# Splitting a weight tile one engine operation at a time, and rebuilding a block of activations ahead of the other lanes of work

## The chip, the cores and the metric

The kernel runs on one core of one Trainium2 chip. The metric is the device time in microseconds (us) of one execution. The core has five engines that follow their own queues of instructions: PE (TensorE, the matrix products), DVE (VectorE), ACT (ScalarE), POOL (GpSimd) and SP, which here issues the transfers (DMA).

## The reference: what is computed

Two layers (`DEPTH = 2`) of a diffusion backbone with `D_MODEL = 1024` on 640 tokens, 128 of context and 512 latent ones. Cut to what matters:

```
h   = modulate(rmsnorm(x))                      # shift and scale from a map of SiLU(cond)
p   = h @ w_in                                  # columns split over four mixers
o   = concat(pool(p), neighbourhood_attention(p), retention(p), gla(p))
x  += gate * rmsnorm(o @ w_out)
h   = modulate(rmsnorm(x))
x  += gate * rmsnorm((silu(h @ w_g) * (h @ w_u)) @ w_down)
```

All of it is float32. Context tokens read only context; latent tokens start their scans from the final context states.

## The kernel before

**Products.** The 640 tokens stand in the free dimension as two halves of 320 (`HW`), the 1024 channels as eight blocks of 128 partitions (`h0` to `h7`). A float32 operand is held as two rounded parts, hi and lo, in a tile whose second index is 0 or 1; a product takes three matmuls of 128x320 for each 128x128 block of weights: hi by hi, hi by lo and lo by hi. So every weight tile that arrives from memory (`raw`, 512 KB) has to be split before PE can use it: a copy makes hi in `hl[:, 0]`, a subtraction makes lo in `hl[:, 1]`. A step of the bulk work is three such matmuls. In the gate and up products of the FFN (feed-forward network) seven products of sums stand in for eight (`seven`); their weights are sums of quarters of two raw tiles, which four operations make in place (`raw<-raw`) ahead of the copy and the subtraction. A half-sized split has the name `hu`.

**Who decides the order.** The program is written out at build time by Python generators. A planner (`Clock`) keeps, in its own units, until when each engine is planned. `drive` goes round: every lane (a generator of small work, such as one head of a mixer, a norm, or the boundary between two layers) makes one step, unless the planner has DVE or ACT booked beyond the present by more than `BACKLOG = 2500.0`; then `stream.feed()` may split the next weight tile; then the bulk (the dense products) makes one step. The order of the steps is the order of the instructions in each engine's queue. For each subtraction `vg` chooses between DVE and POOL, for each copy `copy` chooses between DVE and ACT, by the planner's state at that moment. So a change of when a step is made changes also which engine does what behind it.

**The stream of weights.** `Stream.load` starts transfers into three raw tiles. `Stream.split` issues all operations of one split at once: two, or six where sums are made. `Stream.feed` decides whether to split now; `Stream.next`, called by the bulk when it needs the tile, splits at once if that has not happened yet.

**The names that matter here.** `z` is the sum of the FFN's or the output projection's partial products (`z<-z,acc` adds a product from PSUM and so frees its tile for PE); `sg`, `u`, `act` are the FFN's gate, up and activation; `sq`, `ssqz` are squares and their sums for a norm, `nps` the norm's product over channels, `r` its inverse root; names that begin with `g` belong to GLA, with `n` to the neighbourhood attention, with `r` (`ro`, `rg`, `rq`) to retention; `hps` is a group norm's product. `boundary` ends a layer and makes the next one's `h` (first `xl<-z,nps`, then the modulation of `xl`, then `h` as hi and lo). `second_block` rebuilds, in the last group of the FFN, the second half of `h0` to `h3` from sums that stood there; it is a lane of 16 steps, and the bulk waits for its flag (`until(("block", l))`) before it uses the second half.

Every operation goes through a recording helper, so all rows name the line of that helper (L234 before, L235 after); the tiles' names tell them apart.

Of the kernel before, what the change touches and what calls it, by code (L numbers as in the profile page):

```python
# [133 lines left out]
BIAS_SMALL = -1000.0  # L134
BIAS_QBD = -400.0
BIAS_CP = -200.0
BIAS_SUM = 0.0
BIAS_SNAP = 400.0
BIAS_START = (-2000.0, 2000.0)
# [195 lines left out]
def emit(ctx, tc, a, o):  # L335
    nc = tc.nc
    clock = Clock()
    V, S, G, PE = (clock.proxy(n, e) for n, e in (("V", nc.vector), ("S", nc.scalar), ("G", nc.gpsimd), ("PE", nc.tensor)))
# [19 lines left out]
    def vg(out, in0, in1, op, bias=BIAS_VG):  # L358
        port = not clock.psum([in0, in1])
        if not port:  # L360
            V.tensor_tensor(out=out, in0=in0, in1=in1, op=op)
            return
        at = max(clock.now(), clock.avail(in0), clock.avail(in1))
        v = clock.free_at("V", port, at) + clock.cost("V", "tensor_tensor", [out], [in0, in1], {})
        g = clock.free_at("G", True, at) + clock.cost("G", "tensor_tensor", [out], [in0, in1], {})
        e = V if v <= g + bias else G
        e.tensor_tensor(out=out, in0=in0, in1=in1, op=op)
# [29 lines left out]
    def spawn(gen, first=False):  # L397
        lanes.insert(0 if first else len(lanes), [gen, 0.0, first])
# [198 lines left out]
    class Stream:  # L597


        def __init__(self):  # L600
            self.raw, self.hl, self.where = {}, {}, {}
            self.nd = self.nr = self.ns = self.nu = 0
            self.limit = 0
            self.used = [0, 0, 0]
            self.size = [3, 5, 2]

# [6 lines left out]
                self.nd += 1  # L613

        def split(self, at_once=False):
            kind, srcs, ends, where, _ = jobs[self.ns]
            self.used[where] += 1
            raw = self.raw[srcs[-1]]
            _, kt, n = items[srcs[-1]]
            if kind == "second":  # L620
                hl = hx[0].tile([128, 2, KT // 2, n], F32R, tag="hu", name="hu", bufs=self.size[2])
                raw = raw[:, KT // 2:]
            else:
                hl = (hx[0] if where else ring).tile([128, 2, kt, n], F32R, tag="hl", name="hl", bufs=self.size[where])
            if kind == "sums":

                g, u = self.raw[srcs[0]], raw
                (g1, g2), (u1, u2) = ((t[:, 0:KT // 2], t[:, KT // 2:]) for t in (g, u))
                for out, x, y, op in ((u2, u1, u2, ALU.add), (u1, g1, u1, ALU.subtract), (g1, u2, g1, ALU.subtract), (g2, g2, g1, ALU.subtract)):
                    vg(out, x, y, op, BIAS_SUM)  # L630
                raw = g
            copy(hl[:, 0], raw, BIAS_VS if at_once else bias[0][0])
            vg(hl[:, 1], raw, hl[:, 0].bitcast(F32), ALU.subtract, 2000.0 if at_once else bias[0][1])
            self.hl[self.ns] = hl
            self.where[hl.tensor.name] = where
            self.ns += 1
            for _ in range(ends):
                self.raw.pop(self.nr)
                self.nr += 1
            self.load()  # L640

        def free(self):
            where, when = jobs[self.ns][3:]
# [5 lines left out]
        def feed(self):  # L649

            self.load()
            if self.loaded() and self.free():
                now = clock.now()
                if clock.avail(self.raw[jobs[self.ns][1][-1]]) <= now + AHEAD and (
                        self.ns - self.nu < 2 or max(clock.t["V"], clock.t["S"]) <= now + BACKLOG):
                    self.split()

        def next(self):
            self.load()
            while self.ns <= self.nu:  # L660
                assert self.free() and self.loaded()
                self.split(True)
            hl = self.hl.pop(self.nu)
            self.nu += 1
            return hl
# [780 lines left out]
    def bulk():  # L1446
# [45 lines left out]
        tb0 = mod_mm(loads.pop(0))  # L1492
        V.tensor_tensor(out=xh(0, 0), in0=xh(0, 0), in1=rr[0], op=ALU.mult)
        V.tensor_tensor(out=xh(1, 0), in0=xh(1, 0), in1=rr[0], op=ALU.mult)
        stream.split()
        mod_end(*order[0], tb0)
        rest(rss[1])
        tb1 = mod_mm(loads.pop(0))
        V.tensor_tensor(out=xh(0, 1), in0=xh(0, 1), in1=rr[1], op=ALU.mult)
        mod_end(*order[1], tb1)  # L1500
        stream.split()
        V.tensor_tensor(out=xh(1, 1), in0=xh(1, 1), in1=rr[1], op=ALU.mult)
        for half in range(2):
            for k in range(2):
# [59 lines left out]
        for l in range(DEPTH):  # L1564
# [413 lines left out]
            for gi, gn in enumerate(GROUPS):  # L1978
# [48 lines left out]
                if last:  # L2027
                    if l == 0:
                        yield from until("mods1")
                    hpool("c", 5)  # L2030
                    free(6)
                    yield from room(2)
                    spawn(second_block())
                    sz = u5([128, 4, HW], "ssqz")
                    ssqs = [[sz[:, i], sz[:, 2 + i]] for i in range(2)]

                    hls = [(stream.next(), stream.next()) for _ in range(2)]
                    hds = []
                    for half in range(2):
                        if half:  # L2040
                            yield from until(("block", l))
                        for k in range(2):
                            yield from ev_ffn(*hls[k], acts[early + k], half)
                            if half:
                                stream.done(*hls[k])
                        if half:
                            lnexp()
                        for i in range(4):
                            if not half:
                                hds.append(stream.next())  # L2050
                            jobs = [(hds[i], 2 * i + m, half) for m in range(2)]
                            if i == 0:
                                yield from dn(jobs)
                            else:
                                for job in jobs:
                                    yield from dn([job])
                            if half:
                                stream.done(hds[i])
                        if half == 0:
                            xls = yield from residual(0, xsrc)  # L2060
                            spawn(boundary(0, zt, ssqs[0], xls, dst, nxt))
                else:
                    for i in range(4):
                        if len(z4) == i:
                            yield from room(1)
                            z4.append(u5([128, 2, TOK], "z"))
                        hl = stream.next()
                        jobs = [(hl, 2 * i + m, half) for m in range(2) for half in range(2)]
                        if i == 0:
                            yield from dn(jobs)  # L2070
                        else:
                            for job in jobs:
                                yield from dn([job])
                        stream.done(hl)
# [137 lines left out]
```

## Time and profile before

| | |
|---|---|
| median of 3 runs | 1692.34 us (1687.68 to 1692.91) |
| profiled execution, time | 1690.33 us |
| its span, first to last instruction | 1688.2 us |
| PE busy | 1598.9 us, 95% |
| DVE busy | 1269.9 us, 75% |
| ACT busy | 637.6 us, 38% |
| POOL busy | 307.4 us, 18% |
| mean granted clock of PE | 0.986 |

The span is 2.1 us shorter than the profiled execution's time, and that time is 2.0 us under the median. PE is the engine to watch: what the change can win or lose is PE's idle time, 1688.2 - 1598.9 = 89.3 us, and the stretches in which its clock is granted at the lower level.

### The profile page before, as it was taken

What the parts mean: (1) busy time and instruction counts of PE and PEld (TensorE: products, weight loads), DVE (VectorE), ACT (ScalarE), POOL (GpSimd) and SP (SyncE); (2) the same over time, 40 slices, a digit from 0 to 9 for tenths busy, and PEclk for the clock granted to TensorE, in tenths of its full rate; (3) what the DMA queues carried; (4) which work ended last, traced back from release to release, by engine and by line L of the source; (5) the groups of instructions that cost most, each with busy time, mean ns of one, the idle gap of its engine ahead of it and who ended that gap; (6) DMA issues with size and microseconds to landing.
All of it is one profiled execution on the core that took longest, in us unless ns stands there. A gap on an engine that the chain in (4) does not pass through costs nothing.

```text
span 1688.2 us, 31042 instructions
## 1 busy us (share of the span) xinstructions
PE 1598.9 (95%) x12400; PEld 1485.6 (88%) x12400; DVE 1269.9 (75%) x2510; ACT 637.6 (38%) x1396; POOL 307.4 (18%) x328
## 2 busy tenths in 40 slices
PE   4999999999999999999989998898999999999996
PEld 2888888999998998999979986778999999999996
DVE  5488767788677878786884588766786878878776
ACT  5346655664311112120543466646643211212132
POOL 0200142033011202010243000331330022111012
PEclk9999999999999999999999998999999999999998
DMA  9332231452454455221441311113421212222222
GB/s 368 129 123 93 95 103 63 162 164 82 158 200 162 172 179 183 97 96 63 135 149 58 102 46 42 50 40 132 139 80 65 74 63 101 80 71 92 71 82 94
DMA packets 80000, 188.15 MB, mean 111 GB/s; under 512 B 7632, under 2 KB 38256, under 8 KB 79856
## 3 DMA queue, kind: packets, MB, share of 16 engines
q1 hardware_dynamic: 79856, 186.17, 32.4%
q8 instruction: 98, 1.61, 0.4%
q14 instruction: 46, 0.38, 0.1%
HBM read 173.42 MB, written 12.71 MB: 110 GB/s over the span
## 4 chain that ended last, share of the span: by engine, by line
PE 71%; DVE 19%; ACT 4%; issue 3%; DMA 2%; POOL 1%; SPq 0%; DVEq 0%; ACTq 0%; POOLq 0%
PE acc L234 52%; PE acct L234 6%; DVE hl L234 5%; PE mps L234 3%; DVE z L234 2%; DVE sg L234 2%; DVE act L234 2%; DVE raw L234 1%; PE nsp L234 1%; PE nps L234 1%; DVE u L234 1%; PE rops L234 1%; DMA raw<-in_wdn 1%; PE gdps L234 1%; ACT sq L234 1%
## 5 line engine op out<-in xcount | busy, mean ns | idle before, releaser
L234 PE MATMUL acc<-h,hl 128*128 128x320 f32 x4800 | 764.8, 314 | 17.4 <-ACT h L234 8.4
L234 PEld LDWEIGHTS acc<-h,hl 128*128 128x128 f32 x4800 | 714.5, 189 | 46.5 <-issue 19.1
L234 PE MATMUL acc<-act,hl 128*128 128x320 f32 x2112 | 323.2, 313 | 12.1 <-DVE z L234 9.0
L234 PEld LDWEIGHTS acc<-act,hl 128*128 128x128 f32 x2112 | 314.5, 190 | 21.2 <-issue 11.5
L234 DVE TENSOR_TENSOR hl<-raw,hl 128x1024 fp32r<-128x1024 f32 (+1 forms) x204 | 251.4, 1241 | 12.6 <-ACT hl L234 8.5
L234 ACT ACTIVATE hl<-raw 128x1024 fp32r<-128x1024 f32 (+1 forms) x115 | 116.7, 1029 | 95.2 <-PE acc L234 44.8
L234 ACT ACTIVATE sg<-sg 128x320 f32<-128x320 f32 x64 | 30.2, 472 | 295.9 <-DVE sg L234 295.9
L234 PE MATMUL acct<-hl,h 128*128 128x256 f32 x960 | 132.4, 290 | 0.0
L234 PEld LDWEIGHTS acct<-hl,h 128*128 128x128 f32 x960 | 119.6, 191 | 8.3 <-issue 6.8
L234 PE MATMUL acc<-th,hl 128*128 128x320 f32 x768 | 118.7, 309 | 1.4 <-DVE hl L234 1.4
L234 PEld LDWEIGHTS acc<-th,hl 128*128 128x128 f32 x768 | 114.0, 188 | 2.4 <-DVE hl L234 1.9
L234 POOL TENSOR_TENSOR hl<-raw,hl 128x1024 fp32r<-128x1024 f32 (+1 forms) x24 | 60.2, 2508 | 256.6 <-ACT hl L234 246.9
L234 DVE CAST hl<-raw 128x1024 fp32r<-128x1024 f32 (+1 forms) x113 | 88.0, 779 | 20.1 <-PE acc L234 18.8
L234 DVE TENSOR_TENSOR z<-z,acc 128x320 f32<-128x320 f32 x160 | 71.3, 480 | 25.0 <-PE acc L234 24.7
L234 DVE TENSOR_TENSOR raw<-raw 128x512 f32<-128x512 f32 x103 | 71.0, 689 | 18.3 <-POOL raw L234 15.7
L234 POOL TENSOR_TENSOR raw<-raw 128x512 f32<-128x512 f32 x25 | 33.7, 1347 | 257.5 <-DVE hu L234 157.4
L234 POOL TENSOR_TENSOR nB<-nT,cst 128x248 f32<-128x248 f32 (+2 forms) x32 | 20.0, 624 | 279.9 <-DVE nsp L234 147.1
L234 DVE TENSOR_TENSOR u<-u,acc 128x320 f32<-128x320 f32 x96 | 46.4, 483 | 29.9 <-PE acc L234 27.6
L234 PE MATMUL acc<-th,hu 128*128 128x320 f32 x384 | 61.6, 309 | 0.0
L234 PEld LDWEIGHTS acc<-th,hu 128*128 128x128 f32 x384 | 57.6, 188 | 0.4 <-issue 0.4
L234 PE MATMUL mps<-mraw,ct 128*32 128x256 f32 x768 | 54.0, 391 | 2.0 <-DVE z L234 1.3
L234 ACT ACTIVATE hu<-raw 128x512 fp32r<-128x512 f32 x31 | 19.4, 626 | 91.8 <-PE acc L234 52.9
(284 smaller groups left out, 1976.0 us busy)
## 6 DMA issues: line engine op xcount, KB each, us to landing
mraw<-in_wmod SPq DMA_DIRECT2D x96, 512.0 KB
raw<-in_wgu SPq DMA_DIRECT2D x88, 512.0 KB
raw<-in_win SPq DMA_DIRECT2D x44, 512.0 KB
raw<-in_wdn SPq DMA_DIRECT2D x32, 512.0 KB
raw<-in_wout SPq DMA_DIRECT2D x16, 512.0 KB
xl<-xd SPq DMA_DIRECT2D x12, 640.0 KB
raw<-in_wdn SPq DMA_DIRECT2D x16, 384.0 KB
xd<-y SPq DMA_DIRECT2D x32, 160.0 KB
```

The costliest lines, as they stand in the source:

```text
L234: x = fn(*args, **kw)
```

## The change

`split` becomes a generator that yields after every operation. `feed` makes one of its steps in each round of `drive`, between the lanes' steps and the bulk's step, and a split that has begun goes on only while neither DVE nor ACT is planned beyond the present by more than `STEP = 2500.0`. `next` runs what is left. The two splits at the start of the program are made whole as before (`whole`). And `second_block` becomes the first lane of the list, which is also exempt from the limit on the backlog.

```diff
+STEP = 2500.0
...
+            self.cur = None
...
                 for out, x, y, op in ((u2, u1, u2, ALU.add), (u1, g1, u1, ALU.subtract), (g1, u2, g1, ALU.subtract), (g2, g2, g1, ALU.subtract)):
                     vg(out, x, y, op, BIAS_SUM)
+                    yield
                 raw = g
             copy(hl[:, 0], raw, BIAS_VS if at_once else bias[0][0])
+            yield
             vg(hl[:, 1], raw, hl[:, 0].bitcast(F32), ALU.subtract, 2000.0 if at_once else bias[0][1])
...
+            self.cur = None
             self.load()
+
+        def step(self, at_once=False):
+            if self.cur is None:
+                self.cur = self.split(at_once)
+            next(self.cur, None)
...
         def feed(self):
 
             self.load()
-            if self.loaded() and self.free():
-                now = clock.now()
+            now = clock.now()
+            if self.cur is not None:
+                if max(clock.t["V"], clock.t["S"]) <= now + STEP:
+                    self.step()
+            elif self.loaded() and self.free():
                 if clock.avail(self.raw[jobs[self.ns][1][-1]]) <= now + AHEAD and (
                         self.ns - self.nu < 2 or max(clock.t["V"], clock.t["S"]) <= now + BACKLOG):
-                    self.split()
+                    self.step()
+
+        def whole(self):
+            n = self.ns
+            while self.ns == n:
+                self.step()
...
             while self.ns <= self.nu:
-                assert self.free() and self.loaded()
-                self.split(True)
+                assert self.cur is not None or (self.free() and self.loaded())
+                self.step(True)
...
-        stream.split()
+        stream.whole()
...
-        stream.split()
+        stream.whole()
...
-                    spawn(second_block())
+                    spawn(second_block(), True)
```

The numbers of matmuls and of operations on weights stay the same; what moves is their order and, by the planner's choices, their engine. Over the whole program POOL has 25 subtractions `hl<-raw,hl` of 128x1024 in place of 21, 7 `hu<-raw,hu` in place of 3, 23 sums `raw<-raw` in place of 25; DVE has 187 such `hl` subtractions in place of 191.

DVE in layer 1, at the end of the first group of `seven` products of the FFN, where the adding of the down products to `z` begins. Before:

```order
L234 TENSOR_TENSOR act_14571<-sg_14827,act_14571 128x320
L234 TENSOR_TENSOR hl_14957<-raw_14852,hl_14957 128x1024
L234 TENSOR_TENSOR hu_14969<-raw_14863,hu_14969 128x512
L234 TENSOR_TENSOR raw_14863<-raw_14863 128x512
L234 TENSOR_TENSOR raw_14863<-raw_14852,raw_14863 128x512
L234 TENSOR_TENSOR raw_14852<-raw_14863,raw_14852 128x512
L234 TENSOR_TENSOR raw_14852<-raw_14852 128x512
L234 CAST hl_14975<-raw_14852 128x1024
L234 TENSOR_TENSOR hl_14975<-raw_14852,hl_14975 128x1024
L234 TENSOR_TENSOR z_14293<-z_14293,acc_14950 128x320
L234 TENSOR_TENSOR z_14293<-z_14293,acc_14951 128x320
```

And now (buffer numbers differ, the place is the same):

```order
L235 TENSOR_TENSOR act_14570<-sg_14826,act_14570 128x320
L235 TENSOR_TENSOR hl_14956<-raw_14848,hl_14956 128x1024
L235 TENSOR_TENSOR hu_14968<-raw_14859,hu_14968 128x512
L235 TENSOR_TENSOR raw_14859<-raw_14859 128x512
L235 TENSOR_TENSOR raw_14859<-raw_14848,raw_14859 128x512
L235 TENSOR_TENSOR raw_14848<-raw_14859,raw_14848 128x512
L235 TENSOR_TENSOR raw_14848<-raw_14848 128x512
L235 CAST hl_14977<-raw_14848 128x1024
L235 TENSOR_TENSOR z_14292<-z_14292,acc_14949 128x320
L235 TENSOR_TENSOR z_14292<-z_14292,acc_14950 128x320
L235 TENSOR_TENSOR z_14292<-z_14292,acc_14951 128x320
```

The subtraction of the split with the sums (`hl_14975`, now `hl_14977`) has left DVE; it stands in POOL's queue, where before the next tile's subtraction (`hl_15052`) stood, which in turn is DVE's now. The third group of the same layer changes in the same way.

ACT at the boundary between layer 0 and layer 1. Before:

```order
L234 ACTIVATE ssqz<-z 128x320
L234 ACTIVATE r_9546<-nps,cst 128x320
L234 ACTIVATE r_9545<-r_9546 128x320
L234 ACTIVATE ssqz<-z 128x320
L234 ACTIVATE sq<-z 128x320 x4
L234 ACTIVATE r_9546<-r_9545 128x320
L234 ACTIVATE sq<-z 128x320 x2
L234 ACTIVATE ssqz<-z 128x320
L234 ACTIVATE hl<-raw 128x1024
L234 ACTIVATE xl<-xl,modt_82,der_83 128x128
L234 ACTIVATE xl<-xl,modt_82,der_83 128x192
L234 ACTIVATE h_123<-xl 128x320
```

And now:

```order
L235 ACTIVATE r_9531<-nps,cst 128x320
L235 ACTIVATE r_9530<-r_9531 128x320
L235 ACTIVATE r_9531<-r_9530 128x320
L235 ACTIVATE ssqz<-z 128x320
L235 ACTIVATE sq<-z 128x320 x6
L235 ACTIVATE xl<-xl,modt_82,der_83 128x128
L235 ACTIVATE ssqz<-z 128x320
L235 ACTIVATE hl<-raw 128x1024
L235 ACTIVATE h_123<-xl 128x320
```

The square that ends the inverse root (`r_9546<-r_9545`, now `r_9531<-r_9530`) has moved ahead of five squares of the second half's products, and one of the two modulations of `xl` is no longer ACT's; the six squares still stand ahead of the first `h`.

DVE in the mixing of layer 0, at one of the splits of the input projection. Before, one split's two operations stand next to each other:

```order
L234 TENSOR_SCALAR rk_1672<-acc_1724 128x320
L234 TENSOR_TENSOR gE_1748<-gE_1748,gqk_232 128x512
L234 COPY qbd0_810<-gE_1748 32x256 x2
L234 COPY_PREDICATED gD_1658<-msk_76,gdps_1800 128x256
L234 CAST hl_1815<-raw_1382 128x1024
L234 TENSOR_TENSOR hl_1815<-raw_1382,hl_1815 128x1024
L234 STREAM_TRANSPOSE modb_1844<-mps_1835 128x256
```

And now there are 46 rows between the copy and the subtraction (`rq_1962<-acc_2059` takes the product that PE makes just before it first uses `hl_1898`):

```order
L235 COPY_PREDICATED gD_1684<-msk_76,gdps_1880 128x256
L235 CAST hl_1898<-raw_1337 128x1024
L235 SCALAR_TENSOR_TENSOR r1_1843<-hps_1840,r1_1843 128x256
...
L235 COPY_PREDICATED gD_2114<-msk_76,gdps_2148 128x128
L235 TENSOR_SCALAR rq_1962<-acc_2059 128x320
L235 TENSOR_TENSOR hl_1898<-raw_1337,hl_1898 128x1024
L235 TENSOR_TENSOR gE_2158<-gE_2158,gqk_232 128x256
```

The subtraction has moved from right behind its copy to right behind the eviction of the product before its own.

The programs can also be compared as a whole. For each split one counts the matmuls on PE between the last product whose eviction stands ahead of the split's last operation and the split's first use. Of 260 splits before, the smallest count is 24, the median 150.5, and 6 are under 40; now the smallest is 1 (`hl_1898`), the next are 11, 13, 27, 28 and 29, the median is 144, and 10 are under 40. In layer 1's mixing, the stretches of PE's queue in which only GLA and attention products stand, with no dense product among them, were 25 and 25 rows long and are now 10 and 35. In the output projection of layer 1 ACT's rows `h<-po` to `h<-go` stand directly behind `rg<-rg`, ahead of the two `hl<-raw` that stood there, DVE's two `hl<-raw,hl` ahead of `ro<-ro,rg` are gone from there and two copies `h<-no` have come to DVE; the last group norm's product on PE stands 18 matmuls earlier.

## Rows read from the trace of the kernel before

**Rows 1.** The page: busy time of each engine, share of the span, instructions.

```profile
span 1688.2 us, 31042 instructions
...
PE 1598.9 (95%) x12400; PEld 1485.6 (88%) x12400; DVE 1269.9 (75%) x2510; ACT 637.6 (38%) x1396; POOL 307.4 (18%) x328
```

**Rows 2.** The page: the chain that ended last, by engine.

```profile
PE 71%; DVE 19%; ACT 4%; issue 3%; DMA 2%; POOL 1%; SPq 0%; DVEq 0%; ACTq 0%; POOLq 0%
```

**Rows 3.** The page's costliest groups: count, busy us, mean ns, idle before them, its releaser.

```profile
L234 DVE TENSOR_TENSOR hl<-raw,hl 128x1024 fp32r<-128x1024 f32 (+1 forms) x204 | 251.4, 1241 | 12.6 <-ACT hl L234 8.5
...
L234 POOL TENSOR_TENSOR hl<-raw,hl 128x1024 fp32r<-128x1024 f32 (+1 forms) x24 | 60.2, 2508 | 256.6 <-ACT hl L234 246.9
...
L234 DVE TENSOR_TENSOR z<-z,acc 128x320 f32<-128x320 f32 x160 | 71.3, 480 | 25.0 <-PE acc L234 24.7
```

**Rows 4.** Windows, PE alone: stretch, length, PE busy (instructions), granted clock, DMA share.

```profile
60.00:300.00 240.00, 238.07 (x2232) 1.00 0.28 91
...
1016.00:1041.00 25.00, 17.83 (x171) 0.80 0.14 45
1053.00:1068.00 15.00, 11.33 (x85) 0.89 0.35 113
```

**Rows 5.** Timeline of DVE around 1350, and a later CAST: start, us, operation, count.

```profile
1348.94 2.79 DVE L234 CAST hl<-raw 128x1024 fp32r<-128x1024 f32 x1
1351.76 1.23 DVE L234 TENSOR_TENSOR hl<-raw,hl 128x1024 fp32r<-128x1024 f32 x1
...
1410.58 0.69 DVE L234 CAST hl<-raw 128x1024 fp32r<-128x1024 f32 x1
```

**Rows 6.** Timeline of POOL, and of PE with its idle time before and the releaser.

```profile
1348.70 2.48 POOL L234 TENSOR_TENSOR hl<-raw,hl 128x1024 fp32r<-128x1024 f32 x1 [29.41 <-ACT hl L234]
...
1354.72 1.55 PE L234 MATMUL acc<-act,hl 128*128 128x320 f32 x9 [2.47 <-DVE z L234]
...
1491.19 1.59 PE L234 MATMUL acc<-act,hl 128*128 128x320 f32 x9 [2.75 <-DVE z L234]
```

**Rows 7.** Timeline of PE at the boundary between the layers.

```profile
870.11 0.64 PE L234 MATMUL acc<-h,hl 128*128 128x320 f32 x1 [6.20 <-ACT h L234]
871.98 0.90 PE L234 MATMUL acc<-h,hl 128*128 128x320 f32 x2 [1.23 <-POOL h L234]
```

**Rows 8.** Timeline of ACT there.

```profile
861.99 0.46 ACT L234 ACTIVATE r<-r 128x320 f32<-128x320 f32 x1
...
867.69 1.04 ACT L234 ACTIVATE hl<-raw 128x1024 fp32r<-128x1024 f32 x1
868.64 0.92 ACT L234 ACTIVATE xl<-xl,modt,der 128x128 f32<-128x128 f32 x2
869.59 0.47 ACT L234 ACTIVATE h<-xl 128x320 fp32r<-128x320 f32 x1
```

**Rows 9.** Timeline of PE in layer 1's mixing, the longest waits.

```profile
1023.62 1.08 PE L234 MATMUL gdps<-qbd,gE 128*32 128x128 f32 x16 [2.52 <-ACT qbd L234]
...
1036.13 1.98 PE L234 MATMUL gops<-gat,gv 128*64 128x128 f32 x16 [2.61 <-ACT gat L234]
...
1094.41 0.53 PE L234 MATMUL ntp<-cst,nS 128*96 128x128 f32 x3 [2.26 <-ACT nS L234]
```

**Rows 10.** Timeline of PE at the output projection of layer 1.

```profile
1156.15 0.42 PE L234 MATMUL acc<-h,hl 128*128 128x320 f32 x1 [2.18 <-ACT h L234]
1158.87 1.43 PE L234 MATMUL acc<-h,hl 128*128 128x320 f32 x4 [2.30 <-DVE h L234]
```

**Rows 11.** Timeline of DVE there.

```profile
1152.83 2.36 DVE L234 TENSOR_TENSOR hl<-raw,hl 128x1024 fp32r<-128x1024 f32 x2 [0.57 <-ACT hl L234]
1155.11 0.89 DVE L234 TENSOR_TENSOR ro<-ro,rg 128x320 f32<-128x320 f32 x2
```

**Rows 12.** Timeline of PE in dense products; a window as in Rows 4.

```profile
899.83 4.42 PE L234 MATMUL acc<-h,hl 128*128 128x320 f32 x29
...
870.00:875.00 5.00, 3.66 (x8) 0.50 0.66 209
```

## The prediction, made before the changed kernel ran

> **What bounds the kernel.** I read the page's first section, the chain, the costliest groups, PE's windows, then the timelines of PE and of the engines that release it. PE is busy for 1598.9 of 1688.2 us [rows 1] and holds 71% of the chain that ended last, DVE 19%, ACT 4% [rows 2]. The matmuls don't change in number, so the change can only work on PE's 89.3 us of idle time and on the clock behind it. Where that time lies is to be seen stage by stage: in the mixing of layer 0, from 60 to 300 us, PE is busy for 238.07 of 240 us at a granted clock of 1.00 [rows 4], and nothing can be won there. The waits are short ones elsewhere: 2.47 and 2.75 us at two of the points where the FFN's down products begin [rows 6], 6.20 + 1.23 us at the boundary between the layers [rows 7], 7.17 and 3.67 us in two stretches of layer 1's mixing (length less busy time [rows 4]), 2.26 us later in it [rows 9], 2.18 + 2.30 us at layer 1's output projection [rows 10]. These are 30.8 us, and each of them ends with a small operation on DVE, ACT or POOL that stood behind work on weights or behind its own chain. I go through them by what the order of the changed program puts there.
>
> **Term 1, the two z points of layer 1: -5.2 us.** PE waits for DVE to add a finished product to z and so to free its tile. DVE comes to it late, since a CAST of weights takes 2.79 us there and a subtraction of 1.23 us follows [rows 5]; an ordinary CAST takes 0.69 us [rows 5]. The long one runs beside a POOL subtraction of 2.48 us that began 0.24 us before it and ended at 1351.18, 0.55 us before the CAST did [rows 5, 6]: it waited for POOL. Now the subtraction that follows the CAST is POOL's and can't begin before the CAST ends, and the one that POOL had there is DVE's, behind the z. So the CAST should take 0.69 us (2.10 won) and the subtraction is gone from ahead of z (1.23 won): 3.3 us, more than either wait, 2.47 and 2.75 [rows 6], so both go. POOL then works for 2.5 us beside the additions to z; these have one operand in PSUM, and their group shows 480 ns in the mean over 160 [rows 3], so I cost that at nothing. If they were held up the gain would be 0; the bounds are 0 and -5.2.
>
> The Trainium skill, page "SBUF — State Buffer", section "Who interferes with whom", has the same as a rule: whichever of a DVE copy in its two-port mode and a GpSimd operation starts first has the shared pair of ports for its whole length, and the other fully blocks. The trace agrees at this place (2.79 against 0.69 us). By that rule the change can also lose: it is the third rival.
>
> **Term 2, the boundary: -1 us.** The first product of layer 1 waits 6.20 us for the first h on ACT, then 1.23 us for its lo on POOL [rows 7]. The square that completes the inverse root comes at 861.99 [rows 8], and the change makes it early. But the first h then still stands behind the six squares, the last sum of squares and a weight copy, which ended at 867.69 + 1.04 = 868.73; only the 0.92 us of modulation between that and 869.59 [rows 8] are off ACT's path. That gives 869.59 - 868.73 = 0.9 us, rounded to 1. Bounds: 0 and -7.4, all of the wait.
>
> **Term 3, GLA in layer 1's mixing: -3 us.** While only small GLA and attention matmuls stand in PE's queue, PE waits for their chain through ACT and DVE, 2.52 and 2.61 us at a time [rows 9], and at a granted clock of 0.80 in the mean [rows 4]. The two stretches had 25 rows each, and cost 7.17 / 25 = 0.29 and 3.67 / 25 = 0.15 us of idle time a row. They now have 10 and 35: -15 x 0.29 + 10 x 0.15 = -2.8, rounded to -3. Bounds: -7.2, the first stretch's idle time gone, and +1.5, only the lengthening.
>
> **Term 4, attention at 1094 us: -1.2 us.** PE waits 2.26 us for a score's softmax on ACT [rows 9]. The lane of this head is some rows further ahead in the new order; I take half, with bounds of 0 and -2.3.
>
> **Term 5, the output projection of layer 1: -3.3 us.** The two waits are for h, on ACT and on DVE [rows 10]. On DVE a wait of 0.57 us and two subtractions of weights, 2.36 us, stand ahead of the gating of the retention's output [rows 11]; both are gone from there, and two copies of h have come to DVE, which at ACT's time for the same shape, 0.47 us [rows 8], is some 0.9 less the overlap, say 0.7: 2.93 - 0.7 = 2.2. The norm's product that starts this chain stands 18 matmuls earlier, which at the pace of 4.42 / 29 = 0.152 us each [rows 12] is 2.7 us and could take the rest. I take the middle of 2.2 and 4.48. Bounds: 0 and -4.5.
>
> **Term 6, splits that end late: +3 us.** Now a split that has begun stops between its operations as long as the planner has DVE or ACT booked ahead. Before, no split ended with fewer than 24 matmuls (3.6 us at 0.152) between it and its first use. Now six stand at 1, 11, 13, 27, 28 and 29. For `hl_1898` PE has to end the product, DVE evicts it (0.48, as z) and subtracts (1.24) [rows 3]: 1.7 us, with nothing to cover them; this is in layer 0's mixing, where PE never waited before. Three have 27 to 29 matmuls, 4.1 us and more, which cover 1.7; the two with 11 and 13 have 1.7 and 2.0 us, which just cover it. I add 1.3 us for operations that queue between: +3. Bounds: 0, and six times the worst that rows show: eviction 0.48 and a POOL subtraction of 2.51 [rows 3], 3.0 us, plus 0.75 us of lower clock, as the window behind the boundary's wait ran at 0.50 [rows 12]: +22.5.
>
> **The block first: 0.** In both layers its first operation stands one place earlier on DVE. The bulk's wait for the block shows no row of its own among PE's waits, since a half of products covers it.
>
> **Sum.** -5.2 - 1 - 3 - 1.2 - 3.3 + 3 = -10.7 us. The profiled execution before took 1690.33 us, 2.1 more than its span; so 1679.6 on its scale, and with the 2.0 us by which it lies under the median, 1681.6.
>
> **Rivals.** A: the waits only move. Speaks for it: in mixing and at the boundary PE waits for a chain of small operations, 2.5 us at a time [rows 9], whose links are as long as before; what leaves one stretch of the queue turns up in the next (10 and 35 rows). Then terms 2 to 5 are 0, and -5.2 + 3 = -2.2 gives 1690. Against it: in term 5 weights do stand in the way on DVE, as rows and not as a chain. B, slower: late splits stall PE at each of the six places, for 3.75 us. Terms 1 to 5 are -13.7; 22.5 - 13.7 = +8.8, 1701. It decides from 13.7 / 3.75 = 3.7, that is four stalls on; five make it slower by what can be measured. For it: `hl_1898` has one matmul of cover, and 10 splits instead of 6 have fewer than 40. Against it: a median of 144 matmuls, near 22 us of cover. C: POOL, with four more subtractions of 128x1024 and four more of half that size, holds up DVE's copies, each by 2.1 us as in rows 5 or about 1.3 by halving POOL's 2.51 us: 4 x 2.1 + 4 x 1.3 = 13.6, if each fell before something that PE waits for; 13.6 - 10.7 = +2.9, 1695. Against it: DVE is busy for 75% [rows 1] and in most places has time to catch up.
>
> **Chances.** My forecast 0.55; A 0.22; B 0.15; C 0.08. A measurement of this kernel can tell about 0.3%, 5.1 us, from no change. My forecast's own range is 1668 (the sum with terms 2 to 5 near their better ends, -24) to 1687 (5.1 under the median). The range that holds 8 in 10 goes from 1668 to 1697, which takes in A and C and the start of B. Faster by over 0.3%: 0.57, the forecast and a little of A; within 0.3%: 0.25, most of A and C; slower: 0.18, B and a little of C.
>
> **What would show it.** Term 1: PE's waits for z in the first and third group of layer 1's FFN are gone and no CAST there takes over 1 us; a CAST of 2.8 us ahead of z would refute it. Term 2: PE's wait at the boundary is about 5 us, not 6.2. Terms 3 and 5: less than 8 us idle in the two GLA stretches together, under 1.5 us at the output projection. Term 6: waits for `hl` among PE's, of 1 to 2 us, first in layer 0's mixing, where PE was busy throughout; if they sum to over 10 us, B holds. The prediction is wrong if PE's idle time doesn't fall by about 10 us from 89.3, or if its busy time rises since the lower clock is granted in longer stretches.

## The result, and the profile after

The changed kernel takes 1682.14 us in the median of 4 runs (1680.16 to 1683.00), against 1692.62 us before: a ratio of 0.9945 (95% interval 0.9932 to 0.9958), faster by 10.5 us in the medians (the ratio by itself is 9.3 us). The forecast was 1681.6 us. That the two are so close is partly luck: two terms of the sum came as said, two were a little larger, one failed, layer 0 lost three times the 3 us that the prediction had put down for losses, and a gain in the FFNs that it did not have made up for these.

The page's first section of the kernel after (compare [rows 1]):

```profile
span 1678.4 us, 31025 instructions
...
PE 1595.3 (95%) x12400; PEld 1482.1 (88%) x12400; DVE 1280.1 (76%) x2505; ACT 632.8 (38%) x1401; POOL 307.9 (18%) x326
```

The span is 9.8 us shorter: PE's idle time fell by 6.2 us (89.3 to 1678.4 - 1595.3 = 83.1), and its busy time by 3.6 us for the same 12400 matmuls, since its clock is at the lower level for less time (mean granted clock 0.989, before 0.986). PE's waits after, by what ended them (total us, times, longest):

```profile
PE acc L235 <- POOL hl L235: 6.1, 2, 3.0
PE gops L235 <- ACT gat L235: 5.5, 4, 2.5
PE acc L235 <- ACT h L235: 5.4, 1, 5.4
PE gdps L235 <- DVE qbd L235: 4.9, 3, 2.5
PE acc L235 <- DVE z L235: 4.3, 3, 1.8
...
PE acct L235 <- DVE hl L235: 2.0, 3, 0.8
...
PE acc L235 <- DVE hl L235: 1.0, 1, 1.0
```

And two groups of them before:

```profile
PE acc L234 <- DVE z L234: 9.0, 4, 2.7
...
PE acc L234 <- DVE hl L234: 1.4, 2, 0.7
```

The waits for `hl`, a split's subtraction that is not done when PE wants the tile, have grown from 1.4 to 6.1 + 2.0 + 1.0 = 9.1 us.

To see where the time went, I number the 9024 matmuls of the dense products in order of time, which is the same in all these kernels up to small exchanges, and compare the start of the n-th in two traces. The differences between one n and a later one are the gain or loss of a stage. In us, after less before:

| stage (dense matmuls) | us |
|---|---|
| start and mixing of layer 0 (to 1125) | +6.6 |
| its output projection, first FFN group (to 2000) | +2.7 |
| rest of its FFN, boundary (to 4750) | -4.2 |
| mixing and output projection of layer 1 (to 6375) | -5.5 |
| FFN of layer 1 (to the end) | -9.4 |
| sum | -9.8 |

One profiled execution stands behind each side. Where two kernels have the same queues, the start of the program differed by up to 1.6 us and the stages behind it by up to 1.1, so smaller differences mean nothing. The expectations further down have +7.3, +2.9 and -5.8 us for the changed kernel's +6.6, +2.7 and -5.5: they count from the first dense product and cut at slightly other places.

Timeline of DVE and POOL at the first z point of layer 1, and of PE (compare [rows 5, 6]):

```profile
1348.56 0.69 DVE L235 CAST hl<-raw 128x1024 fp32r<-128x1024 f32 x1
1349.17 2.86 DVE L235 TENSOR_TENSOR z<-z,acc 128x320 f32<-128x320 f32 x7
1351.95 1.22 DVE L235 TENSOR_TENSOR hl<-raw,hl 128x1024 fp32r<-128x1024 f32 x1
...
1349.48 2.42 POOL L235 TENSOR_TENSOR hl<-raw,hl 128x1024 fp32r<-128x1024 f32 x1 [30.57 <-DVE hl L235]
...
1341.16 11.02 PE L235 MATMUL acc<-act,hl 128*128 128x320 f32 x74
```

The CAST takes 0.69 us in place of 2.79, z follows at once, and PE goes through 74 matmuls with no wait. POOL's 2.42 us lie beside seven additions to z at 2.86 / 7 = 0.41 us each, which are not held up. At the other point, in the third group, the CAST takes 0.69 us too and PE's wait is gone. A third wait for z, near the end of this FFN, stays: 1.93 us before, 1.24 us now.

The boundary between the layers, PE and ACT (compare [rows 7, 8]):

```profile
874.62 0.64 PE L235 MATMUL acc<-h,hl 128*128 128x320 f32 x1 [5.44 <-ACT h L235]
876.32 0.90 PE L235 MATMUL acc<-h,hl 128*128 128x320 f32 x2 [1.06 <-POOL h L235]
...
872.79 0.47 ACT L235 ACTIVATE ssqz<-z 128x320 f32<-128x320 f32 x1 [1.70 <-DVE z L235]
873.17 1.04 ACT L235 ACTIVATE hl<-raw 128x1024 fp32r<-128x1024 f32 x1
874.11 0.45 ACT L235 ACTIVATE h<-xl 128x320 fp32r<-128x320 f32 x1
```

Windows of PE (length, busy, granted clock, DMA share; compare [rows 4]):

```profile
60.00:300.00 240.00, 232.08 (x2183) 1.00 0.27 91
...
1016.00:1041.00 25.00, 23.34 (x260) 1.00 0.21 66
1053.00:1068.00 15.00, 11.23 (x90) 0.89 0.23 81
```

In layer 0's mixing PE, busy for 238.07 us before, is busy for 232.08: 6 us of new idle time. In layer 1's the stretch from 1016 is full now, but its GLA waits stand elsewhere. Waits of PE in both mixings and at the ends of the output projections (compare [rows 9, 10]):

```profile
150.66 0.64 PE L235 MATMUL gdps<-qbd,gE 128*32 128x128 f32 x16 [1.59 <-DVE qbd L235]
...
183.25 0.41 PE L235 MATMUL acc<-h,hl 128*128 128x320 f32 x1 [0.99 <-DVE hl L235]
...
394.14 3.83 PE L235 MATMUL acc<-h,hl 128*128 128x320 f32 x13 [3.03 <-POOL hl L235]
...
999.91 1.18 PE L235 MATMUL gops<-gat,gv 128*64 128x128 f32 x16 [2.52 <-ACT gat L235]
...
1062.21 0.66 PE L235 MATMUL gdps<-qbd,gE 128*32 128x128 f32 x8 [2.53 <-DVE qbd L235]
...
1095.20 0.53 PE L235 MATMUL ntp<-cst,nS 128*96 128x128 f32 x3 [0.56 <-ACT nS L235]
...
1147.54 0.70 PE L235 MATMUL hps<-hsq,cst 128*128 128x256 f32 x2 [1.02 <-ACT hsq L235]
1147.89 10.62 PE L235 MATMUL acc<-h,hl 128*128 128x320 f32 x70
1159.21 0.99 PE L235 MATMUL acc<-h,hl 128*128 128x320 f32 x5 [0.70 <-DVE h L235]
...
1231.77 1.58 PE L235 MATMUL acc<-h,hl 128*128 128x320 f32 x8 [3.03 <-POOL hl L235]
```

The last group norm's product of layer 1 (`hps`) and what PE had behind it before:

```profile
1145.79 0.70 PE L234 MATMUL hps<-hsq,cst 128*128 128x256 f32 x2 [0.40 <-ACT hsq L234]
1146.14 7.83 PE L234 MATMUL acc<-h,hl 128*128 128x320 f32 x51
```

What stood before the first wait in layer 0's mixing after the change, DVE and POOL:

```profile
144.19 0.59 DVE L235 COPY qbd<-gE 32x256 f32<-32x256 f32 x2
...
147.93 2.58 DVE L235 COPY qbd<-gE 32x256 f32<-32x256 f32 x2
...
147.36 2.70 POOL L235 TENSOR_TENSOR hl<-raw,hl 128x1024 fp32r<-128x1024 f32 x1 [83.03 <-DVE hl L235]
```

The same two copies for GLA took 0.59 us a few microseconds earlier; beside POOL's subtraction of weights they take 2.58, and PE waits 1.59 us for them. That is the mechanism of rival C.

### The profile page after: what moved, and what is told of

Same layout as the page of the kernel before. It is cut to its first block, busy times and chain, and to the rows that moved or that the text cites. A ratio compares the mean times of both kernels' runs of the same rounds, so it can differ in the third digit from the quotient of the medians.

```text
span 1678.4 us, 31025 instructions
## 1 busy us (share of the span) xinstructions
PE 1595.3 (95%) x12400; PEld 1482.1 (88%) x12400; DVE 1280.1 (76%) x2505; ACT 632.8 (38%) x1401; POOL 307.9 (18%) x326
## 5 line engine op out<-in xcount | busy, mean ns | idle before, releaser
L235 PE MATMUL acc<-act,hl 128*128 128x320 f32 x2112 | 318.0, 310 | 6.1 <-DVE z L235 4.3
L235 PEld LDWEIGHTS acc<-act,hl 128*128 128x128 f32 x2112 | 310.5, 188 | 13.4 <-issue 6.6
L235 DVE TENSOR_TENSOR hl<-raw,hl 128x1024 fp32r<-128x1024 f32 (+1 forms) x201 | 254.8, 1275 | 11.2 <-ACT hl L235 8.4
L235 ACT ACTIVATE sg<-sg 128x320 f32<-128x320 f32 x64 | 30.2, 472 | 270.0 <-DVE sg L235 270.0
L235 PEld LDWEIGHTS acct<-hl,h 128*128 128x128 f32 x960 | 120.7, 191 | 10.5 <-issue 6.0
L235 POOL TENSOR_TENSOR hl<-raw,hl 128x1024 fp32r<-128x1024 f32 (+1 forms) x27 | 67.0, 2480 | 242.3 <-DVE hl L235 121.0
L235 DVE CAST hl<-raw 128x1024 fp32r<-128x1024 f32 (+1 forms) x115 | 84.0, 731 | 13.0 <-PE acc L235 12.2
L235 DVE TENSOR_TENSOR sg<-sg,u 128x320 f32<-128x320 f32 x64 | 38.3, 599 | 19.7 <-ACT sg L235 17.2
```

The costliest lines, as they stand in the source:

```text
L235: x = fn(*args, **kw)
```

## The experiments

Twelve kernels ran. Each is given by its edit and by its ratio to the kernel before; the table behind them has all stages. Of a thirteenth, the changed kernel with `second_block` at the end of the list again, the rows of every engine stand in the same order as in the changed kernel: with stepwise splits the second part of the change does nothing.

**Term 1 alone.** Kernel before, with:

```diff
-            vg(hl[:, 1], raw, hl[:, 0].bitcast(F32), ALU.subtract, 2000.0 if at_once else bias[0][1])
+            if self.ns in (190, 226):
+                G.tensor_tensor(out=hl[:, 1], in0=raw, in1=hl[:, 0].bitcast(F32), op=ALU.subtract)
+            else:
+                vg(hl[:, 1], raw, hl[:, 0].bitcast(F32), ALU.subtract, 2000.0 if at_once else bias[0][1])
```

> The kernel before with one thing changed: at the two z points of layer 1 (first and third group of the FFN) the subtraction of the split with sums is given to POOL, and the planner gives the next one to DVE. The order of PE and ACT stays that of before, DVE differs in 15 rows, POOL in 5. Theory (term 1: the CAST was held up by POOL, and the subtraction stood ahead of z): both CASTs take 0.7 us in place of 2.79, PE's waits of 2.47 and 2.75 us are gone, -5.2 us, 1687.4 us. Rival (the wait only moves to the next product or to the split that is now later): 0, 1692.6 us.

Measured: 0.9966 (0.9950 to 0.9981), 1685.4 us against 1690.4 in the same comparison, -5.0 us (the interval is 3.2 to 8.5 us). PE's waits for z fall from 9.0 to 3.8 us, by 5.2, and the CAST takes 0.69 us:

```profile
PE acc L234 <- DVE z L234: 3.8, 2, 1.9
...
1350.95 0.69 DVE L234 CAST hl<-raw 128x1024 fp32r<-128x1024 f32 x1
1351.56 2.47 DVE L234 TENSOR_TENSOR z<-z,acc 128x320 f32<-128x320 f32 x6
```

Term 1 is shown, mechanism and size: two subtractions go to POOL, the planner gives the ones behind them to DVE, and PE's and ACT's queues stay as they were.

**Which splits pay.** Three kernels, from the changed one, in `feed`:

```diff
-                    self.step()
+                    (self.step if jobs[self.ns][0] == "sums" else self.whole)()   # sums_only
+                    (self.step if jobs[self.ns][0] != "sums" else self.whole)()   # plain_only
+                    (self.step if self.ns >= 30 else self.whole)()                # not_in_l0
```

> Only the splits with sums (FFN) go one operation at a time; plain and half splits are issued whole as before. Up to the first split with sums every queue is as before. Theory (the stages add up, each split form pays where it stands): the mixing of layer 0 loses nothing (+7.3 in the changed kernel), FFN of layer 0 -2.8, boundary -1.4, mixing of layer 1 0, FFN of layer 1 some -9.4: -13.6, about 1679 us. Rival (the planner deals a new order and each stage comes out by chance): stages whose own splits are whole differ from before by several us either way, above all the mixing of layer 1.

> The opposite: plain and half splits go one operation at a time, splits with sums are issued whole. Up to the first split with sums every queue is as in the changed kernel. Theory (stages add up): mixing of layer 0 +7.3, its output projection +2.9, FFN of layer 0 0, mixing and output projection of layer 1 -5.8, FFN of layer 1 0: +4.4, about 1697 us. Rival (the gain in the FFN comes from the plain splits): FFN of layer 1 still some 9 us shorter, about 1688 us.

> The changed kernel, but the splits of layer 0's input and output projection are issued whole as before. Theory (layer 0's mixing is bound by PE and can only lose, 7.3 us there, since operations of splits and of GLA get in each other's way late): that loss is gone and all else stays as in the changed kernel: 1682.1 - 7.3 = 1675 us. Rival (the planner deals a new order behind any change): layer 0's mixing is as before, but what follows differs from the changed kernel by several us either way, so that the time is anywhere from 1675 to 1688 us.

Measured: 0.9915 (0.9894 to 0.9935), 1.0192 (1.0172 to 1.0212) and 0.9910 (0.9892 to 0.9927). In sums_only the splits with sums bring the gain, 8.1 us in each layer's FFN; in plain_only the plain ones bring none, and without those of layer 0's mixing the loss there is gone. Two of the three agree with stages that add up (1675.9 us, better than the 1679 expected; 1675.3 us for 1675). The third doesn't: with plain splits alone, layer 1 loses 23 us where -6 was expected. Of PE's waits in the whole program, these two groups have 11.05 and 9.4 us in layer 1:

```profile
PE acc L235 <- ACT h L235: 16.7, 2, 11.1
PE acc L235 <- DVE z L235: 11.2, 4, 3.8
```

**The two stops of a split.** From the changed kernel:

```diff
             copy(hl[:, 0], raw, BIAS_VS if at_once else bias[0][0])
-            yield                                                     # lo_with_copy
...
-STEP = 2500.0
+STEP = 1e9                                                            # no_hold
```

> The changed kernel without the stop between a split's copy and its subtraction: plain and half splits are whole again, splits with sums stop after each of the four sums. Theory (in the FFN the gain is that the subtraction leaves the place right behind the copy: term 1 and its like in layer 0): the mixings are as before, FFN of layer 1 gains some 3 us instead of 8.1, of layer 0 some 4: about 1685 us. Rival (the gain is that the four sums let additions to z and activations pass between them): both FFNs gain 8 us as in the kernel with only sums stepwise, about 1676 us.

> The changed kernel with STEP without limit: a split that has begun goes on by one operation in every round, whatever DVE and ACT have booked. Theory (the hold is what moves the subtraction behind z, so term 1 depends on it, and late subtractions in the mixing depend on it too): FFN of layer 1 gains 3 us or less instead of 9.4; mixing of layer 0 loses less than 7.3, say 3: about 1689 us. Rival (the interleaving alone does it, the hold matters little): about 1682 us with the same stages as the changed kernel.

Measured: 0.9930 (0.9908 to 0.9952) and 1.0074 (1.0053 to 1.0095). With copy and subtraction together the FFN of layer 1 gains 2.9 us in place of 8.1, so 5.2 of it hang on the stop between them: the waits for z of before are back, behind a CAST of 2.79 us.

```profile
PE acc L235 <- DVE z L235: 8.6, 5, 2.5
...
1340.02 2.79 DVE L235 CAST hl<-raw 128x1024 fp32r<-128x1024 f32 x1
```

In layer 0's FFN 7.0 of 8.1 stay, so there the stops between the sums are enough. Without the hold the FFN of layer 1 gains only 2.5 us, as expected (a CAST of 2.79 us and the subtraction stand ahead of z again, and PE waits 2.47 us there), and layer 0's mixing loses 3.1 in place of 6.6; but 15 us are lost at layer 0's output projection, which no theory had.

**Why stepwise splits cost time in the mixing.** From the changed kernel, two ways:

```diff
-            vg(..., 2000.0 if at_once else bias[0][1])
+            vg(..., 2000.0 if at_once or self.ns % 130 < 37 else bias[0][1])                        # mix_lo_dve
...
-                if max(clock.t["V"], clock.t["S"]) <= now + STEP:
+                if self.ns - self.nu < 2 or max(clock.t["V"], clock.t["S"]) <= now + STEP:            # urgent
```

> The changed kernel, but in both layers the subtractions of the splits of the mixing, the output projection and the first group of the FFN are kept on DVE, as they were before (the changed kernel gives nine such to POOL in layer 1, five in layer 0). Theory (stepwise splits cost time in the mixing because the planner then gives their subtraction to POOL, which holds up DVE's copies for GLA, 0.59 us becoming 2.58 us, and ends late for PE at the two waits of 3.03 us): layer 0's mixing loses 3 us instead of 7.3, the two waits of 3.03 us are gone, some 1675 us. Rival (it is the interleaving itself that puts GLA's and the splits' operations in each other's way): layer 0's mixing still loses 6 to 7 us, only the two waits go, about 1679 us.

> The changed kernel, but a split that has begun is not held back when fewer than two splits are ready ahead of PE. Theory (it is the hold that makes subtractions late where PE has no stock): PE's waits for hl, 9.1 us in the changed kernel, fall under 3 us, layer 0's mixing loses 3 us or less instead of 7.3, FFN of layer 1 keeps its 9: about 1676 us. Rival (the planner deals the small lanes anew): waits for hl fall, but others take their place, 1682 us or above.

Measured: 1.0051 (1.0035 to 1.0068) and 1.0135 (1.0115 to 1.0156). My theory that POOL's subtractions are the cost did not hold: kept on DVE, they are later still, and layer 0's mixing loses 15 us. The two waits of 3.03 us are 3.63 and 3.62 us now, ended by DVE. PE's waits for `hl` in layer 0's mixing:

```profile
157.04 0.41 PE L235 MATMUL acc<-h,hl 128*128 128x320 f32 x1 [3.11 <-DVE hl L235]
...
175.38 0.41 PE L235 MATMUL acc<-h,hl 128*128 128x320 f32 x1 [2.36 <-DVE hl L235]
...
249.46 0.58 PE L235 MATMUL acct<-hl,h 128*128 128x256 f32 x1 [4.52 <-DVE hl L235]
```

So in mix_lo_dve late subtractions are the cost: these three waits are 10.0 of the 15 us. The waits of 1.59 and 0.75 us for DVE's copies for GLA are gone there, so that much POOL did charge, and it charged less than it took off. In the changed kernel the loss has more parts: waits for `hl` in layer 0's mixing are 1.6 us, those in the GLA chain rose from 0.8 to 5.1 us, and only 2.3 of these go with POOL's subtractions; the cause of the others is open. Lifting the hold when stock is low brings layer 0's mixing to +4.0, in the direction expected, but loses 13.7 us at the output projection and the gain in layer 1's FFN.

**Putting the parts together.** Stepwise for splits with sums and for layer 1's two projections only (`jobs[self.ns][0] == "sums" or 130 <= self.ns < 160`), with the rule of mix_lo_dve (best) and without it (best2):

> Splits with sums one operation at a time everywhere, plain splits so only in layer 1's input and output projection, all others whole; in the mixings, output projections and the first FFN group the subtraction is kept on DVE. Theory (stages add up): both FFNs -8 each as with sums alone, mixing and output projection of layer 1 -5.8 as in the changed kernel, layer 0's mixing 0: some 22 us below before, 1669 us. Rival (layer 1's mixing gained by the order that the planner happened to deal): that stage within 3 us of before or worse, 1673 to 1679 us.

> As the kernel named best, without the rule that keeps subtractions on DVE. Theory (a held subtraction is late whatever engine it gets, and DVE, busy with GLA, makes it later than POOL does): the waits for hl on DVE in layer 1's mixing, 8.4 + 3.0 us in best, fall to some 3 us; that stage gains 6 us as in the changed kernel instead of 4.0; about 1668 us. Rival (POOL's subtractions hold up DVE's copies as much as they save): 1670 to 1672 us.

Measured: 0.9858 (0.9830 to 0.9886), 1670.4 us, which beats both kernels; and 1.0016 (1.0006 to 1.0026), 1694.5 us. The first came as the sum of the stages, the second missed by 26 us. It waits once for 11 us:

```profile
1147.43 0.70 PE L235 MATMUL hps<-hsq,cst 128*128 128x256 f32 x2 [1.80 <-ACT hsq L235]
1159.19 0.63 PE L235 MATMUL acc<-h,hl 128*128 128x320 f32 x1 [11.06 <-ACT h L235]
1161.43 0.90 PE L235 MATMUL acc<-h,hl 128*128 128x320 f32 x2 [1.61 <-DVE h L235]
```

Here the last group norm's product has no dense product behind it any more. In the changed kernel 70 matmuls followed the same product (1147.54 to 1159.21 above), 51 before. From that product to the end of the last wait it is 14.0 us in best2, 13.1 before and 11.7 in the changed kernel: the chain differs by 2.3 us at most, the work that covers it by 10.6 us. All traces together say the same of layer 1: with 70 matmuls of cover PE waits not at all for the first h, with 63 (no_hold) 0.32 us, with 51 2.2, with 45 (mix_lo_dve) 7.3, and with none (plain_only, best2, urgent, after_s2400) 8.7 to 11.1 us.

**How much is the deal.** Two changes of a constant that have no mechanism: `BACKLOG = 2400.0` in the kernel before, `STEP = 2400.0` in the changed one.

> The kernel before with BACKLOG 2400 in place of 2500, a change with no mechanism of its own; the queues of all engines differ from some tens of rows after the start on. If a new deal of the order alone makes several us, stages differ from before by 3 us or more either way, above all the mixings; theory: the mixings scatter by 3 to 8 us, the FFNs (bound by PE) by less than 3, total within 10 us of before, 1682 to 1702 us. Rival (the order is robust): within 3 us of before in every stage.

> The changed kernel with STEP 2400 in place of 2500, again without a mechanism of its own. Theory (the FFN's gain belongs to the stepwise splits with sums, the mixings' share is a matter of the deal): FFN of layer 1 keeps -7 to -10, mixings differ from the changed kernel's +7.3 and -5.8 by 3 us or more; 1674 to 1692 us. Rival (all stages keep their values): 1682 us.

Measured: 1.0073 (1.0054 to 1.0092) and 1.0083 (1.0066 to 1.0100). Of the kernel before, PE's wait at layer 0's output projection, where the last group norm's product now has 12 matmuls of cover, and of the changed one two groups of waits:

```profile
323.15 0.63 PE L234 MATMUL acc<-h,hl 128*128 128x320 f32 x1 [10.19 <-ACT h L234]
```

```profile
PE acc L235 <- DVE z L235: 9.1, 4, 3.8
PE acct L235 <- DVE hl L235: 7.8, 3, 3.9
```

A planner's constant moved by 4% costs 12 us without any change of the method, and 24 us with it: both more than the effect under study. In after_s2400 even the FFN of layer 1 keeps only 1.4 of its 9.4 us, which the theory had as safe.

All stages, us against before (the stages of the first table; the last two columns are PE's whole change from start to end and the ratio):

| kernel | mixing 0 | out 0 | FFN 0 | mixing, out 1 | FFN 1 | sum | ratio |
|---|---|---|---|---|---|---|---|
| changed kernel | +6.6 | +2.7 | -4.2 | -5.5 | -9.4 | -9.8 | 0.9945 |
| two_lo | -0.3 | +1.1 | +0.9 | +0.5 | -4.8 | -2.6 | 0.9966 |
| sums_only | -0.2 | 0.0 | -8.1 | -0.1 | -8.1 | -16.5 | 0.9915 |
| plain_only | +7.5 | +3.4 | +2.0 | +12.8 | +10.0 | +35.7 | 1.0192 |
| not_in_l0 | -0.3 | +1.7 | -3.5 | -3.7 | -9.5 | -15.4 | 0.9910 |
| lo_with_copy | -0.4 | 0.0 | -7.0 | -1.4 | -2.9 | -11.7 | 0.9930 |
| no_hold | +3.1 | +15.0 | -2.6 | +3.0 | -2.5 | +16.1 | 1.0074 |
| mix_lo_dve | +15.0 | +2.6 | -3.9 | +6.5 | -9.6 | +10.6 | 1.0051 |
| urgent | +4.0 | +13.7 | -0.5 | +9.6 | +1.9 | +28.6 | 1.0135 |
| best | 0.0 | 0.0 | -8.6 | -4.0 | -8.7 | -21.2 | 0.9858 |
| best2 | +1.0 | 0.0 | -8.0 | +9.1 | +3.9 | +6.0 | 1.0016 |
| before_b2400 | -2.2 | +16.0 | -2.3 | +1.5 | -0.8 | +12.2 | 1.0073 |
| after_s2400 | +11.3 | +1.5 | -4.0 | +7.9 | -1.4 | +15.2 | 1.0083 |

## Why the prediction was right, and where it was wrong

**Term 1 (-5.2)** was right in mechanism and size: both waits are gone, and two_lo gives -5.0 by this alone. (The waits that the prediction lists at its start add up to 30.2 us, not 30.8; no term hangs on that.)

**Term 2 (-1)** was right: 7.43 us of waiting became 5.44 + 1.06 = 6.50, 0.9 less. The sum of squares, the weight copy and the first h stand on ACT in the order that the prediction read from the program: from the start of the copy to that of the h it is 0.94 us (873.17 to 874.11) in place of 1.90 (867.69 to 869.59).

**Term 3 (-3)** failed; rival A held here. PE's waits of 0.15 us and more in that part of layer 1's mixing sum to 10.8 us before and, without those for `hl`, to 11.4 after. The price per row of PE's queue was the wrong step: the rows moved and the sum of the waits stayed, as rival A says of a chain that is as long as before. The chain itself was not measured.

**Terms 4 (-1.2) and 5 (-3.3)** were right and a little small: 2.26 us became 0.56, and 4.48 became 0.70, so -1.7 and -3.8. Term 4's half had no row behind it, and its size alone is borne out. Both parts of term 5 can be seen: the last group norm's product has 70 matmuls of cover in place of 51, 10.62 - 7.83 = 2.8 us more, and from it to the end of the last wait it is 11.7 us in place of 13.1, 1.4 less where 2.2 was expected. The product itself waits 1.02 us in place of 0.40, which gives 0.6 us back. That cover is what counts, the experiments then showed from the other side.

**Term 6 (+3)** was near in size by luck, and the losses beside it were missed. Waits for `hl` are 9.1 us, 7.7 more than before. Two of them are 3.03 us, the worst price that I had named, but not at any of the six splits that I had named: my count looked at evictions on the engine of the split, and these two subtractions stood on POOL, behind additions for a norm. At `hl_1898`, the one place with no cover, PE waited 0.99 us for 1.7 expected. The two waits of 3.03 us stand in place of waits for h of 1.99 and 1.81 us, so they cost less than they show: 7.7 - 3.8 = 3.9 us is left for the term. But layer 0's mixing and output projection lost 9.3 us. What the prediction had put at nothing there are the waits in the GLA chain, 0.8 us before and 5.1 after, with the 1.59 us of rival C among them; it had set that rival aside because DVE would catch up, and there it could not. The 0.75 us of lower clock in the term's upper bound stand on no row.

**What the sum lacked** is the rest of the two FFNs: -4.2 us in layer 0, of which term 2 has about 1, and -9.4 in layer 1, of which term 1 has 5.2. The short waits for z, act and `hl` there shrink (1.93 us at 1573.88 us became 1.24, one of 0.71 in each layer is gone), and in layer 1 with a stretch of lower clock behind them: the granted clock was 0.67 from 1575 to 1580 us before and is 1.00 at the same place now, from 1567 to 1572. This and the failed terms cancelled: -5.2 - 0.9 + 0.6 - 1.7 - 3.8 is -11.0 without term 6; the mixing and the output projection of layer 0 gave +9.3 back, and the FFNs brought some 7.5 more. By its own last sign the prediction was half right: PE's idle time should have fallen by about 10 us and fell by 6.2, and the other 3.6 us came from its busy time.

**The block first** was right at 0, and more than that: with stepwise splits it changes no row's place.

The larger error is one of kind. The prediction takes the new order as the effect of the method, but order in this kernel is also a deal: the two controls lose 12 and 24 us by a constant moved by 4%. What is shown is term 1's mechanism. For the gain of the splits with sums in layer 0's FFN there is good evidence: 7 to 9 us in all four kernels that have it without stepwise plain splits there. But sums_only, best and best2 have the same queues up to 834 us, so these are two orders and not four, and with stepwise plain splits the gain is 0.5 to 4.2 us. That layer 1's FFN keeps its gain is not shown: of the eight kernels with stepwise sums that have both the stop ahead of the subtraction and a hold, five keep it (-8.1 to -9.6) and best2, urgent and after_s2400 lose it, each with a wait for z of 3.3 us and more. At all three of these waits the subtraction stands right behind its copy and ahead of z once more (2.72 + 1.22 us on DVE in best2, 0.69 + 1.23 in urgent, 0.69 + 3.25 in after_s2400): the stop and the hold are no guarantee of the order that term 1 needs. Left open is why the last group norm of a mixing ends up with 70 dense matmuls behind it or with none; that would need the planner's state, not a trace.

## What to carry to other kernels

When a greedy planner writes the order, run a control that moves one of its constants and has no mechanism, before an effect of half a per cent is put down to the method; here the control was larger than the effect. Judge a change of order by stages, since gains and losses in different stages cancel in the total (-9.4 and +6.6 here), and pin by hand the few places whose mechanism is understood: two subtractions on another engine gave 5.0 us with the queues of PE and ACT untouched. At a stage's end ask how much independent work PE has left behind the last small chain: with 70 matmuls behind it a chain of 11.7 us cost 0.7 us of waits, with none behind it one of 14.0 us cost 12.7.

## What the runs showed of the hardware that was not expected

A copy on only 32 partitions, 256 elements wide, is held up by a POOL subtraction as much as a CAST on 128 partitions: two of them took 2.58 us in place of 0.59, 2.0 us more, where the CAST took 2.79 in place of 0.69, 2.1 more. The additions to z, with one operand in PSUM, ran beside the same kind of POOL operation at 0.41 us each. The Trainium skill, page "SBUF — State Buffer", section "Who interferes with whom", has both as rules (copies can take the pair of ports that GpSimd uses; an instruction with at most one SBUF input, outside the two-port modes, doesn't contend), and the trace agrees.

DVE's own subtractions of weights, with both operands in SBUF, are held up as well, which the prediction left out of rival C. This one, usually 1.24 us, is what PE waited for in the 1.93 us at 1573.88 before:

```profile
1568.83 3.31 DVE L234 TENSOR_TENSOR hl<-raw,hl 128x1024 fp32r<-128x1024 f32 x1
...
1568.14 2.92 POOL L234 TENSOR_TENSOR hl<-raw,hl 128x1024 fp32r<-128x1024 f32 x1 [8.27 <-ACT hl L234]
```

It ends 1.08 us after POOL's operation. In the traces of the fourteen kernels 169 such subtractions took over 1.4 us, and 166 of them ended 1.08 or 1.09 us after an operation of POOL.
